# A tuned 4096³ matmul with leaky ReLU: loads and transposes of A issued apart, transposes ahead of sums, first B rounded on two engines

## Chip, cores, metric

One core of one Trainium2 chip. The metric is device time in microseconds (us) of the whole program. In the profile's lines PE is TensorE (PEld its weight loads), DVE is VectorE, ACT is ScalarE, POOL is GpSimd and SP is SyncE. The granted clock is the share of TensorE's full clock that the throttle let through.

## The reference

```python
def reference(a, b, alpha):            # a, b: 4096 x 4096 float32, alpha = 0.01
    x = np.matmul(a, b)
    return np.where(x > 0, x, alpha * x)
```

## The kernel before

All matmuls are bf16, 128 x 128 weights by 512 columns. The work is cut into "steps" of 64 matmuls: one group of eight 128-row chunks of K, four row tiles of A, two column halves of B. The first 8 steps share one 1024-column strip of B for two halves h of A (512 rows each) and are ordered so that work can begin on the first chunks. Their sums leave PSUM for an SBUF tile `part` three times (`spill`). From the ninth step on, four steps accumulate in PSUM without a break.

The first A tiles are rounded on DVE, turned by TensorE into PSUM, and copied out by ACT and DVE, half each. Later A comes in through GpSimd's DMA queue (which rounds) and is turned by DVE:

```python
def take(what, i):                                   # the first step's operands
    if what == "b":
        nc.scalar.copy(b0[:, i, :], b_in[i // 4][:, i % 4, :])
        return
    nc.vector.tensor_copy(a_rounded[:, i, :], a_in[:, i, :])
    cols = a_rounded[:, i, :].rearrange("m (p c) -> m c p", c=KC)
    for c in range(KC):                              # two PSUM banks per A tile
        nc.tensor.transpose(turned[i, c // 4][:, c % 4, :], cols[:, c, :], ident)
    for half, copy in ((0, nc.scalar.copy), (1, nc.vector.tensor_copy)):
        copy(a0[...], turned[i, half]...)            # cut
...
for i in range(1, len(steps)):                       # the other seven steps
    ...
    for quarter in range(4):
        if last:
            todo = [(quarter, c) for c in range(KC)]                                # by row tile
        else:
            todo = [(mt, c) for c in (2 * quarter, 2 * quarter + 1) for mt in range(MT)]  # by chunk
        ... # the matmuls of todo
        if last:
            spill(t, h, quarter, banks)              # sums leave PSUM: DVE
        quarter_of(following, quarter)               # fetch AND transpose of the next A: DVE
```

## Time and profile before

| | before |
|---|---|
| median when the prediction was made | 1789.75 us (3 runs, 1787.66 to 1790.19) |
| profiled execution | 1787.44 us, span 1785.7 us |
| floor: 8192 matmuls x 0.2158 us | 1768 us |
| second step begins (65th matmul, counted in the trace) | 25.24 us |
| seventh and eighth step begin | 94.31 and 110.51 us |
| last matmul begins | 1781.71 us |

A step without a gap takes 64 x 0.2158 = 13.81 us. The seventh takes 16.20: that is the hole of 2.38 us. The stages' table (columns: stage, length, busy time and count of PE, weight loads, DVE, ACT, GpSimd, then granted clock, DMA share, GB/s) shows the clock:

```profile
4.31:7.72 3.41, 1.00 (x10) 0.56 (x8) 1.65 (x3) 1.63 (x2) 0.00 (x0) 1.00 1.00 380
7.72:11.14 3.42, 2.90 (x13) 1.56 (x14) 1.20 (x2) 2.22 (x3) 0.00 (x0) 0.50 1.02 411
11.14:14.55 3.41, 3.30 (x21) 1.63 (x20) 2.04 (x3) 1.99 (x3) 2.99 (x5) 1.00 1.02 416
```

### The profile page before, as it was taken

Reading aid. Unit: us, or ns where it says so; the run is one execution under the profiler, and the core shown is the slowest. Engines: PE = TensorE matmul, PEld = TensorE weight load, DVE = VectorE, ACT = ScalarE, POOL = GpSimd, SP = SyncE. Lnnn points to the kernel's source line nnn. Section 1 sums busy time; section 2 is a strip of 40 time slices with the busy share of each in tenths; the row PEclk is TensorE's granted clock in tenths of the full one; section 3 lists DMA queues with packets and bytes.
Section 4 is the critical chain, followed back from the end, with each engine's and each line's share of the span. In section 5 each row is a group of like instructions: output and inputs, shape, how many; then the busy total and the mean of one; then the engine's idle time right before and its main releaser. Section 6 shows DMA issues by size and latency. Waiting matters only on the chain.

```text
span 1785.7 us, 18129 instructions
## 1 busy us (share of the span) xinstructions
PE 1775.6 (99%) x8232; PEld 805.0 (45%) x8232; DVE 153.8 (9%) x112; ACT 155.5 (9%) x270; POOL 360.9 (20%) x663
## 2 busy tenths in 40 slices
PE   9999999999999999999999999999999999999999
PEld 4444444444444444444444444444444444444444
DVE  4530000023000000003200000000220000000000
ACT  3010000000000000000000000000000000000001
POOL 5630210333002020043201202014320110301000
PEclk9999999999999999999999999999999999999999
DMA  9994562987139165397703917449760481835511
GB/s 260 198 251 97 114 141 77 190 129 123 48 87 194 51 114 123 87 199 129 117 36 94 189 48 136 100 100 203 128 120 16 110 173 48 163 73 120 116 48 47
DMA packets 147021, 214.06 MB, mean 120 GB/s; under 512 B 12801, under 2 KB 76289, under 8 KB 146945
## 3 DMA queue, kind: packets, MB, share of 16 engines
q0 software_dynamic: 126208, 139.50, 48.2%
q10 hardware_dynamic: 17856, 65.02, 9.3%
q1 hardware_dynamic: 2880, 8.39, 1.2%
q8 instruction: 64, 1.05, 0.2%
q14 instruction: 13, 0.10, 0.0%
HBM read 285.21 MB, written 67.11 MB: 197 GB/s over the span
## 4 chain that ended last, share of the span: by engine, by line
PE 99%; DMA 0%; DVE 0%; SPq 0%; issue 0%; ACT 0%; DVEq 0%
PE ps L120 99%; DMA a_in<-in_a_dram 0%; DVE at L105 0%; SPq L215 0%; PE turned L232 0%; SPq L213 0%; DVE part L199 0%; DVE a_rounded L229 0%; ACT o L307 0%; DVEq L105 0%
## 5 line engine op out<-in xcount | busy, mean ns | idle before, releaser
L120 PE MATMUL ps<-bt,at 128*128 128x512 bf16 x8192 | 1769.8, 379 | 2.2 <-DVE at L105 2.2
L120 PEld LDWEIGHTS <-at 128*128 128x128 bf16 x8192 | 801.6, 98 | 969.1 <-DVE at L105 2.7
L117 POOL DMA_DIRECT2D bt<-in_b_dram x408 | 217.3, 539 | 1095.9 <-PE ps L120 973.7
L307 ACT ACTIVATE o<-ps 128x512 f32<-128x512 f32 x240 | 130.7, 595 | 1524.5 <-PE ps L120 1450.0
L105 DVE STREAM_TRANSPOSE at<-a 128x1024 uint32<-128x1024 uint32 x62 | 123.0, 2020 | 1136.0 <-PE ps L120 1123.6
L104 POOL DMA_DIRECT2D a<-in_a_dram x248 | 142.5, 581 | 194.7 <-DVE at L105 138.7
L199 DVE TENSOR_TENSOR part<-ps,part 128x512 f32<-128x512 f32 x32 | 20.6, 685 | 43.9 <-PE ps L120 43.9
L202 ACT ACTIVATE o<-part 128x1024 f32<-128x1024 f32 x8 | 8.5, 1057 | 79.5 <-DVE part L199 68.3
L227 ACT CAST bt<-b_in 128x1024 bf16<-128x1024 f32 x8 | 8.1, 1044 | 1.3 <-DMA b_in<-in_b_dram 1.3
L232 PE MATMUL turned<-ident,a_rounded 128*128 128x128 bf16 x32 | 3.1, 250 | 3.0 <-DVE a_rounded L229 2.9
L197 ACT COPY part<-ps 128x512 f32<-128x512 f32 x8 | 4.4, 593 | 14.0 <-PE ps L120 14.0
L195 DVE COPY part<-ps 128x512 f32<-128x512 f32 x8 | 5.0, 691 | 0.2 <-PE ps L120 0.2
L232 PEld LDWEIGHTS <-a_rounded 128*128 128x128 bf16 x32 | 2.6, 151 | 4.6 <-DVE a_rounded L229 4.6
L82 PE MATMUL ps<-w 128*128 128x512 bf16 x8 | 3.4, 607 | 1.2 <-DVE x L78 1.2
L234 ACT COPY at<-turned 128x512 bf16<-128x512 bf16 x4 | 2.9, 730 | 7.2 <-PE turned L232 7.2
L229 DVE CAST a_rounded<-a_in 128x1024 bf16<-128x1024 f32 x4 | 2.8, 693 | 5.7 <-DMA a_in<-in_a_dram 5.7
L234 DVE COPY at<-turned 128x512 bf16<-128x512 bf16 x4 | 2.9, 733 | 3.7 <-PE turned L232 3.7
L246 POOL CAST x<-bt 128x1 f32<-128x1 bf16 x1 | 0.5, 533 | 10.3 <-ACT bt L227 10.3
L82 PEld LDWEIGHTS <-w 128*128 128x128 bf16 x8 | 1.0, 138 | 2.9 <-issue 1.7
L79 ACT ACT_TABLE_LOAD x1 | 1.3, 1283 | 0.7 <-PEq L329 0.7
L76 DVE MEMSET w<- 128x256 uint32 x1 | 0.3, 272 | 0.9 <-PEq L329 0.9
masks.py:199 POOL TENSOR_SCALAR_AFFINE_SELECT ident<-ident 128x128 bf16<-128x128 bf16 x1 | 0.3, 287 | 0.1
(7 smaller groups left out, 0.9 us busy)
## 6 DMA issues: line engine op xcount, KB each, us to landing
bt<-in_b_dram POOLq DMA_DIRECT2D x408, 256.0 KB, 7.5
out_dram<-o ACTq DMA_DIRECT2D x124, 512.0 KB, 2.9
a<-in_a_dram POOLq DMA_DIRECT2D x248, 128.0 KB, 5.4
b_in<-in_b_dram SPq DMA_DIRECT2D x8, 512.0 KB, 9.3
a_in<-in_a_dram SPq DMA_DIRECT2D x4, 512.0 KB, 6.9
out_dram<-o SPq DMA_DIRECT2D x8, 256.0 KB, 2.0
```

The source lines that it names most:

```text
L82: nc.tensor.matmul(wp, w[:, :P], w, start=True, stop=True)
L104: nc.gpsimd.dma_start(a16[32 * q:32 * q + 32], src.rearrange("(g i) w -> i g w", i=32))
L105: nc.vector.transpose(dst.rearrange("p c m e -> p c (m e)").bitcast(U32).rearrange("p c (g i) -> p g c i", g=8), a16.rearrange("p g w -> p ...
L117: nc.gpsimd.dma_start(new_b(pi, u)[:, c, :], b_rows(n, u, c))
L120: nc.tensor.matmul(ps, at[mb, h, u][:, c // 2, mt * P:(mt + 1) * P, c % 2], bt[pi, u][:, c, nt * NT:(nt + 1) * NT], start=first, stop=last,)
L195: nc.vector.tensor_copy(kept, banks[mt, nt])
L199: nc.vector.tensor_add(kept, banks[mt, nt], kept)
L202: nc.scalar.activation(o, part[h][:, mt, :], LRELU, alpha=alpha)
L227: nc.scalar.copy(b0[:, i, :], b_in[i // 4][:, i % 4, :])
L232: nc.tensor.transpose(turned[i, c // 4][:, c % 4, :], cols[:, c, :], ident)
L234: copy(a0[:, 2 * half:2 * half + 2, i * P:(i + 1) * P, :].rearrange("p c m e -> p c e m"), turned[i, half].rearrange("p (c e) m -> p c e m ...
L307: nc.scalar.activation(o[:, cols], banks[mt, nt], LRELU, alpha=alpha)
```

## The change

Its intent: take the transposes out of the shadow of the sums, get the first A tiles earlier, and share the rounding of the first B between ACT and DVE. Its core (much is renaming for a general cut of K, which here gives the same four groups of eight chunks; not shown: the last chunk of the first B is loaded in two halves, so that SyncE issues 21 transfers instead of 20):

```diff
+        def fetch():   # four DMAs of one A piece
+        def turn():    # its transpose on DVE; now issued apart
...
-    order = [("a", 0), ("b", 0), ("a", 1), ("b", 1), ("b", 2), ("a", 2), ("b", 3), ("a", 3), ...]
+    order = [("a", 0), ("b", 0), ("a", 1), ("b", 1), ("a", 2), ("b", 2), ("a", 3)] + b3 ... b7
...
-    turned = {(mt, i): psum_pool.tile([P, KC // 2, P], BF16) for mt ... for i in range(2)}
+    turned = [psum_pool.tile([P, kc0, P], BF16, name="turned", tag="ps") for _ in range(MT)]
     if what == "b":
-        nc.scalar.copy(b0[:, i, :], ...)
+        for nt, copy in ((0, nc.scalar.copy), (1, nc.vector.tensor_copy)):
+            copy(b0[:, i, columns(nt)], b_in[i][:, columns(nt)])
...
+        if n == 0:
+            for _ in range(4):                        # four more warm-up matmuls
+                nc.tensor.matmul(wp, w[:, :P], w, start=True, stop=True)
-        if (what, i) == ("b", 3): nc.gpsimd.tensor_copy(x[:, :1], b0[:, 2, :1])   # gate of GpSimd's DMAs
+        if (what, i) == ("b", 4): nc.gpsimd.tensor_copy(x[:, :1], b0[:, 4, :1])
...
+        head = 0 if h else kc // 2 if last else kc    # by chunk up to head, then by row tile
+        where = [0, 3]                                # the next step's two transposes
+            for piece, turn in enumerate(following):
+                if where[piece] == g:
+                    turn()                            # ahead of
+            if leaves is not None:
+                spill(t, h, leaves, banks)            # the sums
```

## The prediction

> **What bounds the kernel now.** I first read the page's busy shares, then the costliest groups.
>
> ```profile
> span 1785.7 us, 18129 instructions
> PE 1775.6 (99%) x8232; PEld 805.0 (45%) x8232; DVE 153.8 (9%) x112; ACT 155.5 (9%) x270; POOL 360.9 (20%) x663
> ...
> L120 PE MATMUL ps<-bt,at 128*128 128x512 bf16 x8192 | 1769.8, 379 | 2.2 <-DVE at L105 2.2
> ```
>
> One line of matmuls holds 99% of the span, and everything else is under 21% busy. A busy PE need not be a PE at its peak, so I took its rate from the chain of work that ended last:
>
> ```profile
> 12.82 2.16 PE ps L120 x10
> 14.98 0.50 PE turned L232 x8
> 15.48 78.79 PE ps L120 x365
> ...
> 94.90 0.68 DVE part L199
> 95.58 1.92 DVE at L105
> 97.50 0.05 issue
> 97.55 1684.55 PE ps L120 x7804
> ```
>
> The last piece gives 1684.55 / 7804 = 0.2159 us per matmul (0.2158 start to start in the trace). The floor is therefore 8192 x 0.2158 = 1768 us, and only 1785.7 - 1768 = 17.7 us, 1.0% of the span, is anything else. No reordering of loads and transposes can win 2%. That is the first conclusion, and the verdict rests on it.
>
> The 17.7 us: about 9.1 us before the first real matmul (its start in the trace is 9.10), about 2.6 us of gaps, cold matmuls and transposes up to 15.3 us, 2.4 us at 95 us, and 3.6 us after the last matmul (1782.1 to the end). The waits of PE alone confirm the middle hole:
>
> ```profile
> PE turned L232 <- DVE a_rounded L229: 2.9, 2, 2.2
> PE ps L120 <- DVE at L105: 2.2, 1, 2.2
> PE ps L82 <- DVE x L78: 1.2, 1, 1.2
> ```
>
> The start-to-start gap at 94.96 us is 2.596 us, so it costs 2.596 - 0.216 = 2.38 us. What stood in the way on DVE, from the timeline:
>
> ```profile
> 94.29 1.29 DVE L199 TENSOR_TENSOR part<-ps,part 128x512 f32<-128x512 f32 x2 [2.16 <-PE ps L120]
> 95.50 3.91 DVE L105 STREAM_TRANSPOSE at<-a 128x1024 uint32<-128x1024 uint32 x2
> ```
>
> The transpose of row tiles 2 and 3 of the next step stands behind the last sums of this step, though DVE sat idle 2.16 us before them. PE goes chunk by chunk over all four row tiles, needs tile 2 at its fifth matmul, and waits. Between 15.3 us and there, and from 97.55 us on, no gap over 20 ns is in the trace.
>
> **What the Trainium skill says.** (1) "TensorE: Matmul & The Clock Gate", "Wait — 56ns, not 53.3ns?", gives N / 2.4 GHz + 2.5 ns, 215.7 ns for 512 columns; the trace has 215.8, so there is no slack inside the stream. (2) The same page, "What's actually happening": the clock is half or full, judged in free-running windows of 3413 ns. The stages' table agrees: granted 1.00 in 4.31 to 7.72 us, 0.50 in 7.72 to 11.14, 1.00 afterwards; transposes are 107 ns apart in the cold window and 62 in warm ones, matmuls 427 and 216. (3) "PSUM — Partial Sum Buffer", "PSUM bank collisions raise a hardware error": two engines must not touch one bank in the same quadrant at a time, reads against reads included. The kernel before keeps the halves of a transposed tile in two banks, and its two copies do overlap (ACT at 8.92, DVE at 9.35 us, 0.73 us each). (4) "VectorE: DVE Perf Modes", "Why PSUM operands drop a tier": DVE copies from SBUF can use two read ports. Here 1024 elements take 693 ns from SBUF, 512 take 691 ns from PSUM.
>
> **The change, part by part.**
>
> *Transposes ahead of the sums.* In the built program the second transpose of every following step stands before the sums of row tile 2, and for the step at 95 us the PE order is now row tile by row tile, so tile 2 is needed 6.9 us (32 x 0.2158) after the step begins. DVE reaches that transpose about 10.4 + 1.3 us into the step before, which lasts 13.8. It delays the sums of tiles 2 and 3 by at most 2 us, and their banks are wanted only at 6.9 and 10.4 us. Gain: the whole hole, **-2.38 us**. The steps that go by chunk need all eight banks within 1.5 us; their last copy or sum ends 0.9 to 1.3 us after the step, so no new hole there.
>
> *Loads.* The fetches now run ahead limited by five buffers, not by quarters of a step. DMA serves one A piece per 0.68 us and one B piece per 1.25 us (landing to landing): 5.5 us for an A step, 10 for a B step. Adding these up from the first fetch, every step's data lands before it is used: no gain, no loss.
>
> *The start.* New order: A2 fourth after the first, A3 sixth (one place earlier each). Loads land every 1.28 us from 4.9 us (in the trace A1 at 7.46, A2 at 11.33, A3 at 13.91), so A3 now lands near 12.6, 1.3 us earlier. But 52 matmuls, not 46, remain after A3's transposes, 6 x 0.216 = 1.3 us more. Even if A3 were taken at once the gain is about 0.1 us.
>
> It will not be taken at once. All eight chunks of a turned tile now share one bank, and in the built program DVE's copy of the second half waits for ACT's copy of the first, not for PE; and DVE also rounds half of each B chunk between two A tiles. So each A tile puts a serial chain on DVE: cast 0.69, transposes with latency 0.85, ACT copy 0.78, DVE copy 0.73, half of B 0.38 (estimated from 693 ns for 1024): 3.43 us, against 2.56 us between A tiles. From the first B half's end at 8.0 us (a0 landed 4.56; cast to 5.27; copies to 7.6; plus 0.38) A1's cast begins at 8.0, A2's at 11.4, A3's at 14.85, its transposes near 15.5. Then 0.52 + 52 x 0.2158 = 11.74: the first step ends at 27.2 us. Before: 15.31 + 46 x 0.2158 = 25.24. Loss: **+2.0 us**.
>
> *The gate of GpSimd's loads* moves from chunk 2's rounding (11.5 us) to chunk 4's (ACT reaches it at about 17.5, done 18.1). Then 0.53 for the gate's copy, four issues of 0.6, 4.6 to 4.8 from issue to landing with empty queues (the load issued at 20.73 landed at 25.35), so the first A of the second step lands near 25.4 and is transposed (2.04) by 27.5. The second step starts at about 27.6, not 27.2: **+0.4 us**.
>
> *Four more warm-up matmuls* fill 5.9 to 6.8 us, where PE is idle. They may keep the clock full in 7.7 to 11.1. Nothing on the path above is PE-bound there; a cold window would add 0.3 to 0.5. The tail is unchanged.
>
> Sum: -2.38 + 2.0 + 0.4 = **about 0**, 1789.8 us.
>
> **Rivals.** (a) *The start holds*: if DVE's chain is shorter than I make it (copies overlap after all, or B halves fall into its gaps), the first step ends at 25.2 and only the hole counts: 1789.75 - 2.4 = 1787.3. For it: the change was made to gain, and DVE is idle over half of the first 12 us before. Against: the wait is in the program, and ACT and DVE cannot share a bank. (b) *The second step waits*: the gate opens late, DVE stands in the transpose ahead of the copies that free banks, 1 to 2 us more than above: 1791.5. For it: 4.6 us from issue to landing. Against: the queue is then free of the startup loads, which made the same loads take 8 us before. (c) *The clock drops* once in the first 15 us on the thinner stream of matmuls: +0.5 to 1.5. (d) *A new hole at a step boundary*, since sums now stand behind transposes that may wait for a DMA: 1 to 3 us. My reckoning of landings speaks against it.
>
> **Range and chances.** I shade the sum of 1789.8 towards (a): 1789.4. The three runs before spread 2.5 us, so 1786.6 covers (a) with some luck, 1792.0 covers (b) or (c). Two per cent is 36 us: faster is ruled out by the floor, and slower would need the clock to fall for hundreds of microseconds, which no part of this touches.
>
> **What would show it.** Right: no wait of PE for the transposes near 95 us; DVE's copies of turned tiles starting when ACT's end; A3's transposes near 15.5 and the second step at 27 to 28 us; afterwards one stream at 0.216. Wrong: A3's transposes near 13.4 and a second step at 25.3 (rival a); a PE gap over 1 us at the second step (b); half clock after 11 us (c); any PE gap between 30 and 125 us (d).

## The result, and the profile after

The change: 1787.65 us median of 4 runs (1787.14 to 1788.5); before, then with 4 runs: 1788.87. The ratio is 0.9994, interval 0.9976 to 1.0011: the same within 2%. A ratio here is taken over the runs of the same rounds, so it is not quite the ratio of the medians. Later, with 5 runs of the change and 9 of the kernel before, it was 0.9991 (0.9977 to 1.0005).

The two profiled executions differ as follows (starts counted in the trace):

| us | before | after | difference |
|---|---|---|---|
| second step begins | 25.24 | 26.88 | +1.64 |
| seventh step begins | 94.31 | 95.96 | +1.65 |
| eighth step begins | 110.51 | 109.77 | -0.74 |
| last matmul begins | 1781.71 | 1780.97 | -0.74 |
| the span ends | 1785.67 | 1785.36 | -0.30 |

The hole won 2.38 us, the start gave 1.64 back, and the end gave back another 0.44. That last part is not the engines' work. From the begin of the last matmul to the landing of the last store it is 3.0 us in both. Then SyncE goes through its closing waits, about 0.06 us each. In the kernel before, the last store's landing is the last of eight such waits, and the span ends 0.92 us after it; after the change it is the first of the eight, and the span ends 1.35 us after it. All nine traces with 21 transfers of SyncE have 1.34 to 1.35 us there, all four with 20 have 0.91 to 0.92. That the extra transfer is the reason was not tested by itself. The waits of PE in the profile after (engine and line, waited for: us, times, longest):

```profile
PE turned L264 <- DVE a_rounded L261: 4.0, 4, 1.6
PE ps L84 <- DVE x L80: 1.2, 1, 1.2
PE ps L148 <- ACT at L267: 0.4, 1, 0.4
```

The wait for DVE's transpose at 95 us is gone; the wait for rounded A tiles has grown from 2.9 to 4.0 us. Around 95 us the DVE timeline after shows the transpose (93.69) ahead of four sums instead of behind them:

```profile
92.49 1.29 DVE L225 TENSOR_TENSOR part<-ps,part 128x512 f32<-128x512 f32 x2 [0.44 <-PE ps L148]
93.69 2.05 DVE L121 STREAM_TRANSPOSE at<-a 128x1024 uint32<-128x1024 uint32 x1
95.65 2.46 DVE L225 TENSOR_TENSOR part<-ps,part 128x512 f32<-128x512 f32 x4
```

And the chain that ended last (start, length, what) now begins with a ladder that the chain before did not have; one rung of it:

```profile
7.77 0.61 DVE a_rounded L261
8.38 0.05 issue
8.43 0.72 PE turned L264 x8
9.15 0.02 issue
9.18 0.74 ACT at L267
9.91 0.02 issue
9.94 0.73 DVE at L267
10.67 0.30 DVE bt L259
10.97 0.61 DVE a_rounded L261
```

Cast, eight transposes, ACT's copy, DVE's copy, half of B, next cast: 10.97 - 7.77 = 3.20 us per A tile (3.30 and 3.21 for its neighbours), though A tiles land every 2.56 us. DVE's copy (9.94) starts when ACT's (9.18 + 0.73) ends. In the kernel before, the two copies of a tile overlapped:

```profile
8.92 0.73 ACT L234 COPY at<-turned 128x512 bf16<-128x512 bf16 x1 [1.46 <-PE turned L232]
9.35 0.73 DVE L234 COPY at<-turned 128x512 bf16<-128x512 bf16 x1 [1.17 <-PE turned L232]
```

### The profile page after: what moved, and what is told of

The parts are those of the page before. It is cut to its first block, busy times and chain, and to the rows that moved or that the text cites. A ratio compares the mean times of both kernels' runs of the same rounds, so it can differ in the third digit from the quotient of the medians.

```text
span 1785.4 us, 18146 instructions
## 1 busy us (share of the span) xinstructions
PE 1775.7 (99%) x8236; PEld 804.6 (45%) x8236; DVE 155.8 (9%) x120; ACT 152.0 (9%) x270; POOL 361.4 (20%) x663
## 3 DMA queue, kind: packets, MB, share of 16 engines
q8 instruction: 64, 1.05, 0.2%
## 4 chain that ended last, share of the span: by engine, by line
PE 99%; DVE 0%; DMA 0%; ACT 0%; issue 0%
PE ps L148 99%; DMA a_in<-in_a_dram 0%; ACT at L267 0%; DVE at L267 0%; PE turned L264 0%; DVE a_rounded L261 0%; DVE bt L259 0%; ACT o L360 0%
## 5 line engine op out<-in xcount | busy, mean ns | idle before, releaser
L225 DVE TENSOR_TENSOR part<-ps,part 128x512 f32<-128x512 f32 x32 | 20.3, 683 | 30.4 <-PE ps L148 30.4
L259 ACT CAST bt<-b_in 128x512 bf16<-128x512 f32 x8 | 4.5, 617 | 0.0
```

The costliest lines, as they stand in the source:

```text
L225: nc.vector.tensor_add(kept, banks[mt, nt], kept)
L259: copy(b0[:, i, columns(nt)], b_in[i][:, columns(nt)])
```

## Experiments

The start of the first step differs between executions of the same program, for two reasons that the traces show: the granted clock, and when the A tiles land (A0 to A3 are the first four); the landing of A1 sets when its cast on DVE can begin. So each profile is read with both (us; in some traces 2% of the matmul records are missing, and starts are then good to 0.2 us). The half-clock windows are those of the trace's clock records; these begin at 3.9 to 6.9 us, and before them matmuls are 427 ns apart, which is half clock too.

| kernel | A1 cast | 2nd step | 7th step | 8th step | 7th lasts | half clock |
|---|---|---|---|---|---|---|
| before | 7.49 | 25.24 | 94.31 | 110.51 | 16.20 | 7.7 to 11.1 |
| after | 7.68 | 26.88 | 95.96 | 109.77 | 13.81 | none |
| hole only, on before | 8.41 | 26.83 | 96.00 | 109.82 | 13.82 | 7.4 to 14.2 |
| two banks | 7.70 | 25.32 | 94.39 | 108.20 | 13.81 | none |
| B on ACT | 8.13 | 27.54 | 96.62 | 110.44 | 13.82 | 10.7 to 14.1 |
| no extra warm-up | 7.92 | 28.87 | 97.95 | 111.76 | 13.81 | 9.1 to 15.9 |
| sums first | 8.59 | 28.71 | 97.78 | 111.59 | 13.81 | 9.7 to 16.5 |
| chunk order | 8.75 | 29.01 | 98.08 | 112.60 | 14.52 | 10.3 to 17.1 |
| both undone | 7.80 | 27.43 | 96.51 | 114.30 | 17.79 | 99.6 to 103.0 |
| early gate | 7.54 | 26.72 | 95.79 | 109.60 | 13.81 | none |
| warm-up only, on before | 8.03 | 25.71 | 94.78 | 112.66 | 17.88 | 98.4 to 101.8 |
| warm-up and hole, on before | 7.59 | 25.45 | 94.52 | 108.33 | 13.81 | none |
| after again | 7.96 | 27.14 | 96.20 | 110.02 | 13.82 | none |

What each reason costs can be read off. With the change's start at full clock, the second step begins 19.2 us after A1's cast (after, early gate, after again, and both undone less its wait, see experiment 8); with two half-clock windows it is 20.1 (sums first) and 20.3 (chunk order). With the start of the kernel before, it begins 11.3 us after A3 lands (before, 9 and 10), with one half-clock window or none, and 12.1 us in experiment 1 with its two. So of the 1.8 and 2.1 us by which 5 and 6 are later than the change, 0.9 and 1.1 were there at A1's cast; the rest goes with the clock.

### 1. Only the transpose moved, in the kernel before

```diff
+            if i == 5:
+                quarter_of(following, quarter)
             if last:
                 spill(t, h, quarter, banks)
-            quarter_of(following, quarter)
+            if i != 5:
+                quarter_of(following, quarter)
```

> Kernel before with one edit: in the sixth step (h0, chunk group 3) the transposes of the next step's A stand ahead of the sums of the same row tile. Theory (the hole at 95 us was only the place of one transpose in DVE's order): the transpose starts near 92.1 us instead of 95.5, ends before the step's last sums at 94.3, the 2.4 us gap of PE at 95 us is gone, every step up to the seventh starts as before (second step 25.24 us), and the last matmul starts 2.3 to 2.4 us earlier, at 1779.3 us; time about 2.3 us shorter than before, and about 1.6 us shorter than the change. Rival (the change needed its other parts, such as the separate fetches or the row-tile order, to remove the hole): a gap of over 1 us stays.

Measured: 1786.05 us median of 5 (1785.32 to 1786.75), ratio to before 0.9979 (0.9967 to 0.9992). The timeline of DVE:

```profile
92.54 1.29 DVE L199 TENSOR_TENSOR part<-ps,part 128x512 f32<-128x512 f32 x2 [2.17 <-PE ps L120]
93.74 2.04 DVE L105 STREAM_TRANSPOSE at<-a 128x1024 uint32<-128x1024 uint32 x1
95.99 1.29 DVE L199 TENSOR_TENSOR part<-ps,part 128x512 f32<-128x512 f32 x2 [0.21 <-PE ps L120]
```

The transpose fills the time in which DVE had waited for PE, delays no sum, and the seventh step lasts 13.82 us. The rival fell: one line moved in the kernel before takes the whole hole. The expected last matmul (1779.3) was missed, 1781.01, because the second step came 1.59 us late in this execution. A3 had landed 0.85 us later (14.76 instead of 13.91), and there were two half-clock windows; that part of the expectation had taken landings and clock for constant. The median is 3.7 us under that of the kernel before in the same rounds, which is more than the hole; experiment 7 shows what can add to the hole, but it was not seen in these runs.

### 2. Two banks for the halves of a turned tile

```diff
-    turned = [psum_pool.tile([P, kc0, P], BF16, ...) for _ in range(MT)]
+    turned = {(pair, side): psum_pool.tile([P, 2, kc0 // 2, P], BF16, ...)
+              for pair in range(MT // 2) for side in range(2)}   # side: half of the chunks
```

> Changed kernel, but the two halves of each turned tile lie in two PSUM banks again (four tiles, each holding one half of two row tiles, so no more banks than the change uses). Theory (the start lost 1.64 us to the serial chain on DVE, made by the shared bank): DVE's copies start within 0.1 us of ACT's, A3's transposes start near 13.3 us instead of 14.84, the matmuls of the first step would end near 25.0, and the second step is then held by the gated loads of A until about 25.4; second step at 25.3 to 25.7 us instead of 26.88, last matmul about 1.3 us earlier than in the change. Rival (the halves of B on DVE make the chain, the bank does not matter): A3's transposes stay at 14.5 or later.

Measured: 1786.0 us median of 5 (1785.6 to 1786.45), ratio to before 0.9979 (0.9965 to 0.9993). The timelines of DVE and of ACT:

```profile
7.70 0.69 DVE L265 CAST a_rounded<-a_in 128x1024 bf16<-128x1024 f32 x1 [0.56 <-DMA a_in<-in_a_dram]
9.19 0.73 DVE L272 COPY at<-turned 128x512 bf16<-128x512 bf16 x1 [0.79 <-PE turned L269]
9.82 0.41 DVE L263 CAST bt<-b_in 128x512 bf16<-128x512 f32 x1
10.25 0.69 DVE L265 CAST a_rounded<-a_in 128x1024 bf16<-128x1024 f32 x1
```

```profile
8.95 0.73 ACT L272 COPY at<-turned 128x512 bf16<-128x512 bf16 x1 [1.88 <-PE turned L269]
```

DVE's copy starts 0.24 us after ACT's (expected within 0.1), not 0.76, and does not wait for its end. A rung is 10.25 - 7.70 = 2.55 us, the pace at which the A tiles land (7.68, 10.23 and 12.79). A3's transposes start at 13.56 us instead of 14.84, the second step at 25.32 instead of 26.88, the last matmul at 1779.40 instead of 1780.97. The shared bank was the cause of the lost start: shown, since nothing else was changed. The expected limit by GpSimd's loads did not bind, though narrowly: their gate waits for ACT, which was also freed (it opened at 16.05 us, not 17.38), and the transposed A was ready at 25.08.

### 3. B rounded on ACT alone

```diff
-            for nt, copy in ((0, nc.scalar.copy), (1, nc.vector.tensor_copy)):
-                copy(b0[:, i, columns(nt)], b_in[i][:, columns(nt)])
+            nc.scalar.copy(b0[:, i, :], b_in[i])
```

> Changed kernel, but each chunk of the first B is rounded whole on ACT, as before. Theory: the DVE chain loses the B half, 0.3 us per A tile, so A3's transposes start near 14.0 us instead of 14.84 and the first step's matmuls would end near 25.8; but the gate of GpSimd's loads waits for ACT, which is no faster, so the second step still waits for its transposed A and starts at about 26.9 us with a gap of about 1 us ahead of it. Rival (the B halves are the whole loss): the second step starts near 25.3.

Measured: second step at 27.54 us, with a half-clock window in the start, so its whole cannot be compared with the change at full clock. One rung ahead of that window can:

```profile
8.13 0.69 DVE L260 CAST a_rounded<-a_in 128x1024 bf16<-128x1024 f32 x1 [0.89 <-DMA a_in<-in_a_dram]
11.03 0.68 DVE L260 CAST a_rounded<-a_in 128x1024 bf16<-128x1024 f32 x1
```

It lasts 11.03 - 8.13 = 2.90 us instead of 3.20, so the B half's share is 0.30 us, as the theory has it. And PE waited:

```profile
PE ps L148 <- DVE at L121: 0.5, 1, 0.5
```

It waited at 26.63 us for the transposed A of the second step, a gap 0.70 us longer than a matmul, as the theory has it (about 1 us). A3's transposes started at 15.10 us, not 14.0, after a later landing of A1 and with the half-clock window. The B halves on DVE are not the whole loss: 0.30 us a rung, where two banks win 0.65.

### 4. Without the four extra warm-up matmuls

> Changed kernel without the four extra warm-up matmuls at 5.8 us. Theory: the granted clock falls to half from about 7.7 to 11.1 us as in the kernel before, A1's transposes take 0.107 us each instead of 0.062, and the chain, so also A3's transposes and the second step, comes 0.3 to 0.5 us later: second step at 27.1 to 27.4 us. Rival (the extra matmuls do nothing for the clock, or the chain hides it): second step at 26.9 as in the change.

(The edit takes the four matmuls at `n == 0` away.) Measured: second step at 28.87 us, two half-clock windows. The sign was right, the size not: 2.0 us later than the change, where 0.2 to 0.5 was expected. I had counted on one window, and not on this wait, for the transposed A of the second step, which makes its first matmul begin 1.27 us after the one ahead, 1.05 us more than a matmul:

```profile
PE ps L148 <- DVE at L121: 0.9, 1, 0.9
```

The windows:

```profile
5.70:9.11 3.41, 0.93 (x14) 0.79 (x13) 1.63 (x3) 1.20 (x2) 0.00 (x0) 1.00 1.00 363
9.11:15.94 6.83, 6.19 (x25) 2.46 (x23) 3.27 (x6) 2.41 (x4) 0.00 (x0) 0.50 1.02 407
```

One execution does not show that the warm-ups are the reason: experiments 5 and 6 had them and fell to half clock as well.

### 5 to 7. The two ways out of the hole, in the changed kernel

Transpose behind all sums of the sixth step (5), seventh step by chunk (6), both (7):

```diff
-                if where[piece] == g:
+                if where[piece] == g and not (i == 5 and piece == 1):   # 5 and 7
                     turn()
             if leaves is not None:
                 spill(t, h, leaves, banks)
+        if i == 5:
+            following[1]()                                              # 5 and 7
...
-        head = 0 if h else kc // 2 if last else kc
+        head = kc if i == 6 else 0 if h else kc // 2 if last else kc    # 6 and 7
```

> Changed kernel, but the second transpose for the seventh step stands behind all sums of the sixth, as in the kernel before; the seventh step still goes row tile by row tile. Theory (either part of the change fills the hole alone): the transpose runs at about 1.3 to 3.3 us after the seventh step has begun, row tile 2 is wanted 6.9 us after, no gap of PE there. Rival (the place of the transpose decides): a gap near 2.4 us.

> Changed kernel, transposes ahead of sums, but the seventh step goes chunk by chunk over all four row tiles, as before. Theory: the second transpose ends about 0.2 us before the seventh step begins, so A is there, but it has pushed the last four sums to end about 2.2 us after the step's begin, and a step by chunks wants the eighth bank 1.5 us after its begin: a gap of about 0.7 us in the first eight matmuls of the step, waited for on DVE's sums, not on its transposes. Rival (banks are no matter): no gap.

> Changed kernel with both of the last two edits: the transpose behind all sums, and the seventh step chunk by chunk. Both theories: the hole of the kernel before is back, a gap of 2.2 to 2.6 us some four matmuls into the seventh step. If it is not, something else in the change (the separate fetches) had filled it.

Measured: (5) no gap, the seventh step lasts 13.81 us, though the transpose starts at 98.97 us, 1.2 us after the step has begun. (6) 14.52 us, two gaps that together exceed two matmuls by 0.71 us (expected about 0.7). (7) a gap of 2.57 us, 2.36 over a matmul, as before. The waits of PE, of (6) and then of (7):

```profile
PE ps L148 <- DVE part L225: 0.4, 2, 0.2
```

```profile
PE ps L148 <- DVE at L121: 2.5, 2, 2.2
```

(The second wait in (7) is ahead of the second step; see experiment 8.) So in the changed kernel the row-tile order alone fills the hole; the earlier transpose alone leaves 0.7 us, because it puts four sums off and a step by chunk wants all eight banks at once. The place of experiment 1, ahead of the last row tile's sums only, has not even that.

(7) also showed something that I had not expected. Its seventh step lasts 17.79 us, 3.98 more than without the hole. The stages:

```profile
97.16:99.60 2.44, 0.38 (x2) 0.00 (x0) 2.44 (x4) 0.00 (x0) 0.54 (x1) 1.00 1.08 291
99.60:103.02 3.42, 3.29 (x8) 1.20 (x9) 3.42 (x3) 1.06 (x1) 1.07 (x2) 0.50 1.08 292
```

Directly after the hole one window ran at half clock: 3.98 - 2.36 = 1.6 us more. The hole of the kernel before can cost 2.4 or 4 us, and its profiled execution showed only the first.

### 8. The gate of GpSimd's loads as early as before

```diff
-        if (what, i) == ("b", 4): nc.gpsimd.tensor_copy(x[:, :1], b0[:, 4, :1])
+        if (what, i) == ("b", 3): nc.gpsimd.tensor_copy(x[:, :1], b0[:, 2, :1])
```

> Changed kernel, but GpSimd's loads are let go after chunk 2 of B is rounded, as before, not after chunk 4. Theory: in the change the transposed A and the end of the first step met within 0.1 us, so the gate alone changes nothing while the DVE chain stands: the transposed A is there at about 25 us or earlier, and the second step starts at 26.8 us at full clock (later by 0.5 to 2 us where the clock falls to half in the first 15 us), with no gap ahead of it. Rival (the gate was the bound): the second step starts at 25.3 to 25.9 us.

Measured: the second step at 26.72 us, no gap ahead of it, at full clock. The first transpose of A on DVE came 3.1 us earlier than in the change (21.64 instead of 24.74 us) and nothing followed from it:

```profile
21.64 2.03 DVE L121 STREAM_TRANSPOSE at<-a 128x1024 uint32<-128x1024 uint32 x1 [1.82 <-DMA a<-in_a_dram]
```

In this execution and in the change's the gate was not the bound, but the margin is thin. In experiment 7, whose start is that of the change and at full clock, the gate opened only 0.09 us later (17.47 us), yet the loads came later and the transposed A was ready at 27.37 us instead of 26.82. PE waited for it, 0.48 us more than a matmul from start to start:

```profile
27.43 2.77 PE L148 MATMUL ps<-bt,at 128*128 128x512 bf16 x12 [0.32 <-DVE at L121]
```

### 9 to 11. Warm-up alone, warm-up with the moved transpose, and the change again

Both of the first two start from the kernel before, with four warm-ups after the first A tile and the turned tiles packed by halves as in experiment 2 (the warm-up's bank must stay free); the second has the edit of experiment 1 too. All three ran in the same rounds.

> Kernel before with the change's four extra warm-up matmuls after the first A tile and nothing else that matters (the turned tiles share four banks by halves, so that the warm-up bank stays free; the hole at 95 us is left). Theory (a part of what the change gains is clock, not schedule): fewer executions have windows of half clock in the first 15 us, so the granted clock is more often 0.999 or 1.000 than before (0.997 to 0.999), and the median is 0.5 to 1.5 us shorter than before; the hole of 2.4 us stays, and where it draws a half-clock window after it, 1.7 us more. Rival (the clock is chance alone): the clocks spread as before, and so do the times.

> The same and the one transpose moved ahead of the sums (the edit of the first experiment). Theory: both gains add, the second step starts at 25.0 to 25.3 us at full clock, no gap at 95 us, last matmul near 1779.2, median 1785.3 to 1786.2 us, 1.2 to 2 us shorter than the change. Rival (the change's other parts earn something too): not shorter than the change.

> The changed kernel once more, so that it is timed in the same rounds as the two others. Theory: 1787.1 to 1788.5 us as before, clock 0.998 to 1.000, and against the kernel before 0.05 to 0.15 per cent shorter, because the kernel before loses more to half clock than its profiled execution, the best of its runs, showed.

| | median us | runs | range | granted clock of the runs |
|---|---|---|---|---|
| before | 1789.34 | 9 | 1787.41 to 1790.60 | 0.997 x2, 0.998 x2, 0.999 x5 |
| warm-up only | 1789.53 | 5 | 1787.71 to 1789.63 | 0.999 x3, 1.000 x2 |
| warm-up and moved transpose | 1785.30 | 5 | 1784.83 to 1785.99 | 1.000 x5 |
| the change | 1787.39 | 5 | 1787.10 to 1787.49 | 1.000 x5 |

Warm-up alone failed its expectation: the clock is higher, the median is not shorter (ratio 1.0, 0.9988 to 1.0013). Its profile has full clock in the start and the half window after the hole:

```profile
98.39:101.80 3.41, 3.41 (x10) 1.22 (x8) 1.48 (x1) 0.05 (x1) 1.65 (x4) 0.50 1.26 277
```

The three runs at 0.999 took 1789.53 to 1789.63 us and the two at 1.000 1787.71 and 1788.34, which fits one such window (1.7 us) in three of five; only the profiled one is seen.

With the hole gone as well, the version of experiment 10 takes 1785.30 us: ratio 0.998 to before (0.9967 to 0.9992), and 1785.34 / 1787.34 = 0.9989 by means against the change, with ranges that do not meet. Within 2% all four are the same, but in these rounds it beats both kernels, by 0.1 to 0.2%. Its span is 2.13 us shorter than the change's in the profiled executions: 1.69 at the second step (25.45 against 27.14; expected 25.0 to 25.3) and 0.44 after the last matmul, where it has the 20 transfers of the kernel before. It does so by keeping the order of the kernel before and adding one moved transpose, four matmuls and another packing of the turned tiles.

## Why the prediction was right, point by point

The mechanisms of the hole and of the start were right; that the sum came so near zero was partly luck. In the profiled pair the terms are -2.38, +1.64, 0 and +0.44, where the prediction had -2.38, +2.0, +0.4 and 0: two costs too large and one overlooked.

- **The floor.** Right: nothing but 1% could be won, and the result is within 2%. The time fell in the range, 1.75 us below the point. (In the split of the 17.7 us, the part up to 15.3 us is 15.31 - 9.11 - 18 x 0.2158 = 2.3 us of gaps, not 2.6; nothing rests on it.)
- **The hole, -2.38 us.** Right in size: the seventh step went from 16.20 to 13.81 us. Not seen: that the hole can also draw a half-clock window of 1.6 to 1.7 us. The experiments show too that either half of the mechanism would do, or nearly (5 and 6).
- **The start, +2.0 us.** The mechanism was right and is shown by experiment 2. The size was 1.64 (1.69 between experiments 10 and 11): a rung lasts 3.20 us, not 3.43, because consecutive DVE instructions start before the one ahead has ended (half of B takes 0.41 us, yet its piece of the chain is 0.30 long). A3's transposes came at 14.84, not 15.5. Of these 0.7 us, 0.3 were lost again: a term left out is that PE, in the middle of the remaining matmuls, waits for DVE's copy of A3's second half (in the chain, the copy from 16.36 to 17.11 and the next matmul at 17.15).
- **The gate, +0.4 us.** It was 0 in the profiled execution: the transposed A was ready at 24.74 + 2.08 = 26.82 us, the first step ran out at 26.88, and experiment 8 shows that an earlier gate wins nothing there. But the path was seen rightly: in experiment 7 it cost 0.48 us, with the same start.
- **The tail, "unchanged".** Wrong: +0.44 us, in SyncE's closing waits.
- **New holes at later steps (rival d).** None, as reckoned.
- **Extra warm-ups and the clock (rival c).** The size was about right, 0.3 to 0.5 us for a cold window: two of them cost 0.9 to 1.1 us in experiments 5 and 6. What failed was to read the clock and the landings of one execution as the kernel's. The profiled execution of before, 1787.44 us, was one of its fastest; its median later was 1789.3 to 1789.7. The point of 1789.4 took 1789.75 as base and added a sum of zero, where the traces of the pair give -0.30; the rest of the difference is not measured term by term.

What stays open: how much the four warm-ups do for the clock. Of the timed runs without the hole, those with warm-ups had 1.000 in 17 of 19 (change, twice; two banks; experiment 10) and the kernel without them (experiment 1) in 2 of 5; yet three of the four single looks with them (3, 5, 6) fell. In these three A1 landed at 8.11 to 8.72 us, in all profiled executions with warm-ups that kept full clock in the start at 7.29 to 8.00. That fits the closing list, where the clock falls after windows in which PE was idle long enough, since PE waits for late tiles; but nobody varied the landing on purpose, nor is it known why it differs.

## What to carry to other kernels

When a kernel sits at its floor, list the gaps of the bounding engine one by one, and for each ask what stands in the way in the order of the engine that it waits for: often it is one instruction, and moving that one is worth more than a new order of everything. When two engines are to share a job, see that their inputs lie in different PSUM banks, or the sharing becomes a relay. And compare clock records and landings before comparing starts: one profile can be the lucky one. Last, compare also what comes after the last matmul: here 0.44 us of a difference of 0.74 was lost there.

## What the Trainium skill lacked or had wrong

- "TensorE: Matmul & The Clock Gate", "What's actually happening" and the table of goals: it asks for an idle window, or a gap of more than about 3 us, before the clock falls. Here a PE wait of 2.2 us was enough (experiment 7: full clock to 99.60 us, then half for 3.42 us). The same wait in the kernel before drew none. The busy share of PE in each of the clock's own windows (3.41 us, counted from the first clock record) tells the two apart: 40% ahead of the fall in experiment 7, while in the kernel before the wait was split over two windows of 67 and 68%. In all traces, in the windows at full clock that end before the last matmul, half clock followed the eight with 27 to 42%, and none with 51% or more. The highest that was followed by half clock (experiment 3) and the lowest that was not (after, here cut 0.04 us late):

```profile
7.30:10.72 3.42, 1.45 (x12) 0.77 (x12) 1.02 (x2) 1.16 (x3) 0.00 (x0) 1.00 1.01 376
```

```profile
7.72:11.14 3.42, 1.75 (x12) 0.77 (x12) 1.85 (x5) 1.20 (x2) 0.00 (x0) 1.00 1.02 408
```

  The page gives no share of busy time; these runs put it between 42% and 51%.
- The same page, "Part 4: PE-mode transpose": it has full clock not engage for transposes, and says that they do not count as busy in the same way. Here they follow the clock: about 62 ns from start to start at full clock, 107 at half. And they count: with them the windows part cleanly at 42 and 51%, without them the one of experiment 7 that fell has 40% and the one of after that did not has 35%.
- "PSUM — Partial Sum Buffer", "PSUM bank collisions raise a hardware error": it states the rule, and the programs here keep it by a wait; what the wait costs is not there. Here it is 3.20 instead of 2.55 us per turned tile (2.55 is the pace of the loads, so the wait may cost more), and 1.56 us on the second step.
